# Sums of weight blocks made by accumulating DMAs on GpSimd's queue instead of by VectorE, in a transformer layer on Trainium2

## The chip, the cores and the metric

The kernel runs on one core of a Trainium2 chip, as one launch. The metric is device time in microseconds (us): the median of several executions. One further execution is recorded by the hardware profiler; its trace is what the prediction reads. The engines of the core each work through their own queue of instructions in a fixed order and wait on semaphores: TensorE (PE; its weight loads are listed as PEld), VectorE (DVE), ScalarE (ACT), GpSimd (POOL) and SyncE (SP). Before the change, SyncE issues every DMA of the kernel.

## The reference

One layer on a sequence of 1024 positions with 1024 channels, in float32:

```
h = rms_norm(x)
proj = h @ w_in                      # 1024 x 7168: q, k, v, gates, LRU branch, merge gates
A: rotary(q, k), chunkwise retention, group norm, swish gate, @ w_ret_o
B: causal conv (4), RG-LRU scan, times gelu(y), @ w_lru_o
x = x + (sigmoid(gate_A) * A + sigmoid(gate_B) * B) @ w_out
up = rms_norm(x) @ ffn_w_up          # 1024 x 6144
x = x + (gelu(conv3(gate)) * val) @ ffn_w_down
out = rms_norm(x)
```

## The kernel before, in words

**Tiles and units.** All large matrix products are cut into units (class `Job`). A unit computes a 256 x 1024 block of a product, as four quarters of 128 x 512, one per PSUM bank, from four weight blocks `A11`, `A12`, `A21`, `A22` of 128 x 512 values (256 KB each) and eight pairs of operand tiles. Float32 accuracy is kept with three passes: `split` (lines 617 to 621 of the kernel before) makes of a tile a rounded high half `hi` (a cast on ScalarE, L619) and a low half `lo = src - hi` (a subtraction on VectorE, L620), and TensorE multiplies hi by hi, hi by lo and lo by hi (L704 in seven-product units, L684 in plain ones).

**Seven-product units.** Most units use a scheme with seven block products instead of eight (`mm_fast`, Winograd's form of Strassen's). Each product is 12 matmuls of 128 x 512, so a unit is 84. The weight side needs `A11`, `A12`, `A22` and four sums: `S1 = A21 + A22`, `S2 = S1 - A11`, `S3 = A11 - A21`, `S4 = A12 - S2`. `blocks` (from L623) makes them on demand: SyncE loads a block (tile `wr`, L629), VectorE adds (S1 into a tile `ws` at L640, S2 in place at L643, S3 in place over `A11` at L646, S4 in place at L649), then `split` makes the halves. The order of the products in a unit is A11, S1, S2, A12, S3, S4, A22. Three banks X, Y, Z collect them: `keep` (L712, ScalarE) copies a bank to SBUF after the A11, S1 and S2 products, TensorE goes on accumulating on X after its copies, and `total` (L722, VectorE) adds a bank to a kept copy. The A22 product ends the unit and goes from the bank straight to `emit`. The activation side needs four sums T1 to T4, made once per operand by `tsets` or, through DRAM, by `sums_of` (lines 778 to 787).

**Stages.** Input projection: four plain units, then 24 seven-product units from about 103 us on; beside them run rotary embedding, retention heads and LRU blocks, as generators that are advanced after each product. Then the projections of both branches, `w_out` with plain units, FFN up (two plain units, 22 seven-product units from 971 us on) with convolution and gelu (tiles `gc`, stored to `ff_d`), and FFN down (12 seven-product units).

**What sets the order.** `record` writes down all operations; `Prog` then orders each engine's instructions with a list scheduler: each operation has a cost (`cost`), a latest start found backwards from TensorE's order (`plan`), and `forward` walks through time, giving every engine the ready operation with the earliest latest start, as long as one of 100 tile buffers of 128 x 512 is free. TensorE's main order is that of the recording. The instructions are then written in that order, and at run time an engine never passes over a waiting instruction.

Of the kernel before, what the change touches and what calls it, by code (L numbers as in the profile page):

```python
# [205 lines left out]
class Prog:  # L206
# [54 lines left out]
    def cost(self, o, how, n, outs, ins, args, kw):  # L261
# [25 lines left out]
        elif o.eng == "ACT":  # L287
            c = n / 1.2
            func = args[2] if how == "activation" else None
            o.tab = TABLES.get(func)  # L290
            extra = (60 if scal else 0) + (20 if func is not None else 0)
            o.occ, o.lat = c + (52 if ps else 95) + extra, c + (195 if ps else 230) + extra
            if "accum_out" in kw:
                o.occ += 150
                o.lat += 200
            o.occ += 20
        elif how == "dma_start":
            size = math.prod(args[0].shape) * 4
            o.dma = size
            o.occ = 420 if o.eng == "SP" else 800  # L300
            o.lat = 2700
        else:
            o.occ, o.lat = n * 2.0 + 100, n * 2.0 + 200
# [71 lines left out]
    def forward(self, caps):  # L375
# [37 lines left out]
        dma_free = 0.0  # L413
        tab = None
# [27 lines left out]
        def start(o, t):  # L442
            nonlocal dma_free, tab, slip, n
# [6 lines left out]
            if o.dma:  # L450
                arrive = max(t + 700, dma_free)
                dma_free = arrive + o.dma / 262144 * self.TILE
                lat = max(dma_free + 900 - t, 2300.0)
# [120 lines left out]
RATE = 2.5  # L574
SLACK = 45000.0
# [3 lines left out]
class Job:  # L579

    def __init__(self, src, op, emit, post=None, fast=True, pre=None, fetch=None, js=(0, 1, 2, 3)):
        self.src, self.op, self.emit, self.post = src, op, emit, post
        self.fast, self.pre, self.fetch = fast, pre, fetch
        self.js = js


def record(prog, fx):
# [35 lines left out]
    def blocks(jb):  # L623
        raw, blk = {}, {}

        def load(nm):
            if nm not in raw:
                t = get("wr")
                SY.dma_start(t, jb.src(int(nm[1]) - 1, int(nm[2]) - 1))  # L629
                raw[nm] = t  # L630
            return raw[nm]

        def block(nm):
            if nm in blk:
                return blk[nm]
            if not jb.fast or nm in ("A11", "A12", "A22"):
                s = load(nm)
            elif nm == "S1":
                s = raw["s"] = get("ws")
                V.tensor_add(s, load("A21"), load("A22"))  # L640
            elif nm == "S2":
                s = raw["s"]
                V.tensor_sub(s, s, raw["A11"])  # L643
            elif nm == "S3":
                s = raw["A11"]
                V.tensor_sub(s, s, raw["A21"])  # L646
            else:
                s = raw["s"]
                V.tensor_sub(s, raw["A12"], s)  # L649
            blk[nm] = split(s, "w")  # L650
            return blk[nm]

        return block
# [39 lines left out]
    def mm_fast(jb, op):  # L693
# [15 lines left out]
        def keep(ps):  # L709
            u = get("pk")  # L710
            with within(1200.0):
                S.copy(u, ps)  # L712
            return u

        def more(u, m, c):
            if jb.pre is not None and (m, c) in jb.pre:
                with within(3000.0):
                    V.tensor_add(u, u, jb.fetch(m, c))

        def total(u, ps, m, c):  # L720
            with within(1200.0):
                V.tensor_add(u, ps, u)  # L722
# [7 lines left out]
        z = keep(Z)  # L730
# [11 lines left out]
        with within(1500.0):  # L742
            jb.emit(1, 0, X, None)
# [30 lines left out]
    def sums_of(fetch, dst, j):  # L774
# [3 lines left out]
        V.tensor_sub(t, b[0, 1], b[0, 0])  # L778
# [5 lines left out]
        V.tensor_sub(b[1, 1], b[1, 1], t)  # L784
        SY.dma_start(dst[1, j], b[1, 1])
        yield 1.0
        V.tensor_sub(b[1, 0], b[1, 0], b[1, 1])
# [10 lines left out]
    def tsets(op, fetch):  # L798
        for j in range(4):
            b11, b12, b21, b22 = (fetch(n, j) for n in ("B11", "B12", "B21", "B22"))  # L800
            t1, t2 = get("ts"), get("ts")
            V.tensor_sub(t1, b12, b11)
            op["T1", j] = split(t1, "b")
            V.tensor_sub(t2, b22, t1)
# [3 lines left out]
            V.tensor_sub(t2, b21, t2)  # L808
# [141 lines left out]
    def emit_to(d, name, func=None):  # L950
        def emit(m, h, src, unit):
            t = get(name) if unit is None else unit
            if func is not None:
                S.activation(t, src, func)
            elif unit is None:
                S.copy(t, src)
# [3 lines left out]
    def emit_y(n):  # L960
        def emit(m, h, src, unit):
            t = get("y") if unit is None else unit
            S.activation(t, src, AF.Gelu_apprx_tanh)
# [169 lines left out]
    def emit_gate(which, n, scaled):  # L1133
        def emit(m, h, src, unit):
# [5 lines left out]
            S.activation(t, src, AF.Sigmoid, bias=pc("merge_gate_b", 8 * which + 2 * n + m))  # L1140
# [32 lines left out]

    def emit_ret_o(n):
        def emit(m, h, ps, unit):
            t = ojobs[n].fetch(m, h)
            V.tensor_mul(t, ps, t)
# [3 lines left out]
    def emit_lru_o(n):  # L1181
        def emit(m, h, ps, unit):
            g, t = ojobs[4 + n].fetch(m, h)
            V.tensor_mul(g, ps, g)
# [6 lines left out]
    def add(i, emit, post=None):  # L1191
        fast = len(jobs) >= STD_L
        jobs.append(Job(pair_src(w_in, i), h1 if fast else h1u, emit, post, fast=fast))
# [27 lines left out]
    ojobs = [Job(pair_src(w_ro, n), og, emit_ret_o(n), fast=n >= STD_RO, fetch=from_sg(0, n)) for n in range(4)]  # L1221
    ojobs += [Job(pair_src(w_lo, n), u, emit_lru_o(n), fast=n >= STD_LO, fetch=from_sg_t1(n))
# [19 lines left out]
    def emit_out(n):  # L1242
        def emit(m, h, ps, unit):
# [3 lines left out]
            V.tensor_add(t, ps, t)  # L1247
# [26 lines left out]
    def channel_major():  # L1274
# [9 lines left out]
        run([Job(pair_src(w_out, n), mop, emit_out(n), out_post(n), fast=n >= STD_W, js=(0, 1, 3, 2))  # L1284
# [63 lines left out]
    run([Job(pair_src(w_up, i), h2, emit_to(gvs[i], "gv"), up_post(i), fast=i >= STD_U) for i in range(NF)])  # L1348
# [15 lines left out]
    def emit_down(g, t):  # L1364
        def emit(m, c, src, unit):
            if unit is not None:
                acc = unit
            else:
                acc = djobs[4 * g + t].fetch(m, c)
                V.tensor_add(acc, src, acc)  # L1370
# [14 lines left out]
    def final(t, m):  # L1385
# [5 lines left out]
        for c in range(2):  # L1391
# [3 lines left out]
            else:  # L1395
# [4 lines left out]
                 emit_down(g, t), pre=((0, 0), (0, 1), (1, 1)), fetch=from_x1(t))  # L1400
# [98 lines left out]
```

## Time and profile before

| | |
|---|---|
| median of 3 runs | 1625.58 us (1625.5 to 1626.76) |
| profiled execution, its own time | 1628.01 us |
| its span in the trace | 1626.2 us |
| granted TensorE clock, mean | 0.999 |
| DMAs issued by SyncE | 1,054, 268.68 MB |
| VectorE instructions | 2,360 |

A line of the trace's groups reads: source line, engine, operation, output tile <- input tiles by their names in the program, shapes, xcount, then busy us in total, mean ns of one, and the engine's idle time just ahead of these instructions with what ended it. Line numbers are those of the kernel before, unless said otherwise; after the change `split` is L630 and L631, `keep` L735, `total` L749, the accumulating DMA L648.

### The profile page before, as it was taken

How to read it: one execution, taken by the hardware profiler on the slowest of the kernel's cores; microseconds unless marked ns; L12 is line 12 of the kernel's file. 1: busy time of each engine (PE TensorE's matmuls, PEld its weight loads, DVE VectorE, ACT ScalarE, POOL GpSimd, SP SyncE). 2: the span in 40 equal slices, each digit the busy share in tenths (PEclk: the TensorE clock that was granted, in tenths of full speed). 3: DMA queues.
4: the chain of work that ended last, by engine and by line, in shares of the span. 5: the costliest groups of instructions: out<-in, count | busy, mean ns of one | idle time of the engine just before them, and what ended most of it. 6: DMA issues, size and time to landing. Idle time of an engine off the chain costs nothing.

```text
span 1626.2 us, 21515 instructions
## 1 busy us (share of the span) xinstructions
PE 1603.8 (99%) x7204; PEld 1325.8 (82%) x7204; DVE 1294.9 (80%) x2360; ACT 925.9 (57%) x1592; POOL 0.2 (0%) x4
## 2 busy tenths in 40 slices
PE   7999999999999999999999999999999999999998
PEld 6888888888888888788888888888888888888886
DVE  4999668878779898989961599777777787989795
ACT  7764448749755866945430765444444455555564
POOL 0000000000000000000000000000000000000000
PEclk9999999999999999999999999999999999999999
DMA  9223304314225446999450514444444456987762
GB/s 334 85 98 107 88 27 137 106 38 159 76 90 182 150 154 209 320 370 345 136 206 0 174 54 141 151 142 144 148 130 138 146 163 196 335 287 273 271 237 97
DMA packets 167631, 270.04 MB, mean 166 GB/s; under 512 B 16864, under 2 KB 43616, under 8 KB 167520
## 3 DMA queue, kind: packets, MB, share of 16 engines
q1 hardware_dynamic: 167520, 268.68, 49.1%
q8 instruction: 56, 0.92, 0.2%
q14 instruction: 55, 0.45, 0.1%
HBM read 187.87 MB, written 75.50 MB: 162 GB/s over the span
## 4 chain that ended last, share of the span: by engine, by line
PE 91%; ACT 3%; DMA 3%; DVE 2%; issue 1%; SPq 0%; ACTq 0%; DVEq 0%
PE g L704 71%; PE g L684 14%; PE a L1001 2%; PE a L1094 1%; PE a L1093 1%; PE a L1101 1%; DMA bf<-u_d 1%; DMA wr<-w_lo 1%; DMA sg_d<-pk 0%; ACT L1004 0%; PE a L1124 0%; PE a L1087 0%; ACT L1014 0%; ACT lg L1004 0%; PE a L1254 0%
## 5 line engine op out<-in xcount | busy, mean ns | idle before, releaser
L704 PE MATMUL g<-bh,wl 128*128 128x512 f32 x1556 | 612.9, 394 | 0.4 <-DVE wl L620 0.4
L704 PE MATMUL g<-bh,wh 128*128 128x512 f32 x1556 | 612.2, 393 | 0.9 <-ACT pk L712 0.9
L704 PE MATMUL g<-bl,wh 128*128 128x512 f32 x1556 | 612.0, 393 | 0.0
L704 PEld LDWEIGHTS g<-bh,wh 128*128 128x128 f32 x1556 | 292.5, 188 | 60.4 <-ACT pk L712 1.5
L704 PEld LDWEIGHTS g<-bh,wl 128*128 128x128 f32 x1556 | 292.4, 188 | 60.5 <-DVE wl L620 1.2
L704 PEld LDWEIGHTS g<-bl,wh 128*128 128x128 f32 x1556 | 292.5, 188 | 59.5
L620 DVE TENSOR_TENSOR wl<-wr,wh 128x512 fp32r<-128x512 f32 x304 | 205.6, 684 | 19.5 <-ACT wh L619 18.9
L619 ACT CAST wh<-wr 128x512 fp32r<-128x512 f32 x304 | 180.6, 619 | 44.5 <-DVE wr L646 10.6
L722 DVE TENSOR_TENSOR pk<-g,pk 128x512 f32<-128x512 f32 x195 | 133.8, 686 | 81.5 <-PE g L704 80.9
L712 ACT COPY pk<-g 128x512 f32<-128x512 f32 x195 | 114.2, 586 | 139.5 <-PE g L704 136.5
L619 ACT CAST wh<-ws 128x512 fp32r<-128x512 f32 x195 | 120.8, 621 | 127.5 <-DVE ws L643 51.4
L620 DVE TENSOR_TENSOR wl<-ws,wh 128x512 fp32r<-128x512 f32 x195 | 133.2, 685 | 21.5 <-ACT wh L619 20.7
L704 PE MATMUL g<-hh,wl 128*128 128x512 f32 x264 | 102.8, 389 | 0.0
L704 PE MATMUL g<-hl,wh 128*128 128x512 f32 x264 | 102.8, 389 | 0.0
L704 PE MATMUL g<-hh,wh 128*128 128x512 f32 x264 | 102.8, 389 | 0.0
L684 PE MATMUL g<-hh,wh 128*128 128x512 f32 x192 | 76.7, 399 | 9.6 <-ACT wh L619 9.6
L1320 DVE SCALAR_TENSOR_TENSOR gc<-pk,par,gc 128x511 f32<-128x511 f32 x88 | 65.6, 746 | 23.0 <-ACT gc L1317 22.6
L1317 ACT ACTIVATE gc<-pk,par 128x512 f32<-128x512 f32 x44 | 35.9, 815 | 76.0 <-DVE pk L722 75.9
L684 PE MATMUL g<-hl,wh 128*128 128x512 f32 x192 | 76.4, 398 | 0.0
L684 PE MATMUL g<-hh,wl 128*128 128x512 f32 x192 | 76.3, 397 | 0.0
L684 PE MATMUL g<-bl,wh 128*128 128x512 f32 x160 | 63.2, 395 | 0.0
L684 PE MATMUL g<-bh,wl 128*128 128x512 f32 x160 | 63.1, 394 | 0.0
(236 smaller groups left out, 2134.7 us busy)
## 6 DMA issues: line engine op xcount, KB each, us to landing
wr<-w_in SPq DMA_DIRECT2D x112, 256.0 KB, 3.2
wr<-w_up SPq DMA_DIRECT2D x96, 256.0 KB, 3.5
dw<-w_dn SPq DMA_DIRECT2D x96, 256.0 KB, 5.0
ff_d<-gc SPq DMA_DIRECT2D x48, 256.0 KB, 2.5
wr<-ff_d SPq DMA_DIRECT2D x48, 256.0 KB, 5.1
td<-td_d SPq DMA_DIRECT2D x48, 256.0 KB, 5.3
x<-x_d SPq DMA_DIRECT2D x48, 256.0 KB, 5.2
td_d<-dw SPq DMA_DIRECT2D x36, 256.0 KB, 2.0
```

The source lines that it names most:

```text
L619: S.copy(hi, src)
L620: V.tensor_sub(lo, src, hi.bitcast(F32))
L684: PE.matmul(ps[m], w[a][:, c], o[b], start=k == 0 and i == 0, stop=k == 7 and i == 2)
L704: PE.matmul(ps, w[a][:, c], o[b], start=first and n == 0, stop=n == 11, skip_group_check=True)
L712: S.copy(u, ps)
L722: V.tensor_add(u, ps, u)
L1001: PE.matmul(ps, wg[g][a][:, cs], xs[k][b], start=q == 0, stop=q == 5)
L1093: PE.matmul(p2[:, 0:256], qk[0, h][:, bs], rst[cur], start=True, stop=False)
L1094: PE.matmul(p2[:, 0:256], s, v, start=first, stop=True)
L1101: PE.matmul(p3[:, 0:256], kd[h][:, bs], v, start=True, stop=True)
L1317: S.activation(c, src, AF.Identity, bias=pc("ffn_conv_b", i), scale=pc("ffn_conv_w", 48 + i))
L1320: V.scalar_tensor_tensor(c[:, s:], src[:, :TH - s], w, c[:, s:], ALU.mult, ALU.add)
```

## The change

In `blocks`, a unit can now ask for sums by DMA: an accumulating DMA issued from GpSimd adds a weight block from DRAM to a tile in SBUF. An addition is all that is used, so the sums change sign: `S2 = S1 + A11` and so on, with the signs turned on the activation side (`sums_of`, `tsets`), in `keep` (a copy with a scale of 1 or -1), in `total` and in the `emit` functions. The units of the input projection (`ACC_IN`) and of FFN up (`ACC_UP`) have all four sums made in this way; those of the other stages keep VectorE, with the new signs. S1 is made over the loaded `A21`, S2 and S4 on the same tile after it, S3 over `A11`. In each of these 46 units GpSimd issues four DMAs of 256 KB, 184 in all, and each of them waits until both halves of the block that stood in the tile have been made.

```
+ACC_IN = 2
+ACC_UP = 2
+ACC_DN = 0
+ACC_O = 0
...
+        def part(nm):
+            return jb.src(int(nm[1]) - 1, int(nm[2]) - 1)
+
+        def plus(t, nm):
+            G.dma_start(t, part(nm), accum_op=ALU.add)
+            return t
...
-            if not jb.fast or nm in ("A11", "A12", "A22"):
+            if nm[0] == "A":
                 s = load(nm)
-            elif nm == "S1":
-                s = raw["s"] = get("ws")
-                V.tensor_add(s, load("A21"), load("A22"))
-            elif nm == "S2":
-                s = raw["s"]
-                V.tensor_sub(s, s, raw["A11"])
-            elif nm == "S3":
-                s = raw["A11"]
-                V.tensor_sub(s, s, raw["A21"])
+            elif nm == "S3":
+                if jb.acc > 0:
+                    s = plus(raw["A11"], "A21")
+                else:
+                    s = raw["A11"]
+                    V.tensor_add(s, s, raw["A21"])
+            elif nm == "S1":
+                if jb.acc > 0:
+                    s = raw["s"] = plus(load("A21"), "A22")
+                else:
+                    s = raw["s"] = get("ws")
+                    V.tensor_add(s, load("A21"), load("A22"))
+            elif jb.acc > 1:
+                s = plus(raw["s"], {"S2": "A11", "S4": "A12"}[nm])
             else:
                 s = raw["s"]
-                V.tensor_sub(s, raw["A12"], s)
+                V.tensor_add(s, s, raw[{"S2": "A11", "S4": "A12"}[nm]])
...
-        def keep(ps):
+        def keep(ps, scale=1.0):
             u = get("pk")
             with within(1200.0):
-                S.copy(u, ps)
+                S.activation(u, ps, AF.Copy, scale=scale)
             return u
...
         def total(u, ps, m, c):
             with within(1200.0):
-                V.tensor_add(u, ps, u)
+                (V.tensor_sub if m else V.tensor_add)(u, u, ps)
...
-        V.tensor_sub(b[1, 1], b[1, 1], t)
+        V.scalar_tensor_tensor(b[1, 1], t, -1.0, b[1, 1], ALU.mult, ALU.subtract)
```

The scheduler's costs get a line for these DMAs (a higher latency, twice the bytes), so the order of all engines is made anew:

```
-            o.lat = 2700
+            o.lat = 2700 if "accum_op" not in kw else 4500
```

Three places of the new order, which the prediction uses. The names are tiles with a running number: `wr` a loaded weight block, `ws` a sum made by VectorE, `wh` and `wl` the halves of a block, `g` a PSUM bank, `pk` a kept copy, `gc` and `gv` gate and value tiles of FFN up, `lg`, `lth` and `ly` tiles of an LRU block.

**ScalarE, in the middle of FFN up.** Before the change, around the end of one unit and the start of the next (row 1110 takes the A22 product of one unit from its bank, row 1112 keeps the A11 product of the next):

```order
1108 L1317 ACTIVATE gc_10863<-pk_10803,par 128x512
1109 L619 CAST wh_10870<-wr_10850 128x512
1110 L956 COPY gv_10879<-g_10722 128x512
1111 L1323 ACTIVATE gc_10863<-gc_10863 128x512
1112 L712 COPY pk_10904<-g_10877 128x512
1113 L619 CAST wh_10909<-ws_10898 128x512
1114 L619 CAST wh_10927<-ws_10898 128x512
1115 L712 COPY pk_10934<-g_10902 128x512
```

After the change, at the like place (row 1110 takes the A22 product, rows 1106, 1112 and 1117 cast S1, S2 and S4 of one tile, row 1114 casts S3, row 1113 keeps the A11 product):

```order
1106 L630 CAST wh_10817<-wr_10775 128x512
1107 L630 CAST wh_10824<-wr_10801 128x512
1108 L1350 ACTIVATE gc_10830<-pk_10754,par 128x512
1109 L630 CAST wh_10845<-wr_10821 128x512
1110 L983 ACTIVATE gv_10850<-g_10686 128x512
1111 L1356 ACTIVATE gc_10830<-gc_10830 128x512
1112 L630 CAST wh_10867<-wr_10775 128x512
1113 L735 ACTIVATE pk_10873<-g_10842 128x512
1114 L630 CAST wh_10892<-wr_10821 128x512
1115 L735 ACTIVATE pk_10896<-g_10871 128x512
1116 L735 ACTIVATE pk_10918<-g_10842 128x512
1117 L630 CAST wh_10923<-wr_10775 128x512
```

The casts of the sums have moved among the copies out of PSUM, and one of them (row 1112) ahead of the copy that it used to follow. In every second unit the copy still comes first.

**VectorE, in an LRU block of the input projection.** Before the change, where the S4 block of one unit is summed (row 445) and its low half made (row 447); the addition that follows the A12 product of that unit, on bank `g_2873`, is row 467:

```order
443 L620 TENSOR_TENSOR wl_2729<-wr_2599,wh_2720 128x512
444 L722 TENSOR_TENSOR pk_2668<-g_2617,pk_2668 128x512
445 L649 TENSOR_TENSOR ws_2684<-wr_2735,ws_2684 128x512
446 L620 TENSOR_TENSOR wl_2757<-wr_2735,wh_2751 128x512
447 L620 TENSOR_TENSOR wl_2767<-ws_2684,wh_2759 128x512
448 L620 TENSOR_TENSOR wl_2781<-wr_2645,wh_2775 128x512
449 L1052 TENSOR_TENSOR pk_2405<-pk_2405,cos_1545 128x512
```

After the change, from the addition that follows the A12 product (row 418, on bank `g_2857`) to the low half of that unit's S4 block (row 427):

```order
418 L749 TENSOR_TENSOR pk_2773<-pk_2773,g_2857 128x512
419 L1053 TENSOR_TENSOR lg_2802<-lg_2802,lth_2784 128x512
420 L1081 TENSOR_TENSOR qk_2577<-qk_2577,qs_2822 128x512
421 L1055 SCALAR_TENSOR_TENSOR lg_2802<-lg_2758,lg_2802 128x512
422 L1081 TENSOR_TENSOR pk_2404<-pk_2404,qs_2837 128x512
423 L1043 SCALAR_TENSOR_TENSOR lg_2816<-lg_2816,lth_2846 128x512
424 L1057 SCALAR_TENSOR_TENSOR lth_2784<-lg_2758,st,lg_2802 128x512
425 L1044 TENSOR_SCALAR lg_2816<-lg_2816 128x512
426 L1062 TENSOR_TENSOR ly_2723<-ly_2723,lth_2784 128x512
427 L631 TENSOR_TENSOR wl_2920<-wr_2569,wh_2904 128x512
```

The low half has moved from 20 rows ahead of that addition to 9 rows behind it, after a scan (row 424) and other LRU and rotary operations. On TensorE, 8 transposes and 14 matmuls stand between the end of the product on `g_2857` and the first matmul that reads `wl_2920`.

**GpSimd, in FFN up.** Before the change GpSimd has no DMA. After it, its queue holds these and nothing else after the start; each unit is S1 and S2 on one tile (x2), S3 on another, S4 on the first:

```order
119 L648 DMA wr_10775<-w_up 128x512 x2
120 L648 DMA wr_10821<-w_up 128x512
121 L648 DMA wr_10775<-w_up 128x512
122 L648 DMA wr_10938<-w_up 128x512 x2
123 L648 DMA wr_10990<-w_up 128x512
124 L648 DMA wr_10938<-w_up 128x512
```

The sums of the next unit follow the S4 of this one directly, in the one queue.

More of the change, by code (lines that the diff above doesn't have):

```diff
@@ L716, in more @@
             if jb.pre is not None and (m, c) in jb.pre:
+                if jb.where is not None:
+                    with within(3000.0):
+                        G.dma_start(u, jb.where(m, c), accum_op=ALU.add)
+                    return
                 with within(3000.0):
```

89 lines of the change are left out of this document (51 added, 38 removed).

## The prediction, before the result was known

> **What bounds the kernel now.** I read the page's busy times first, then a table of stretches, then the waits of the engine that is busiest.
>
> ```profile
> span 1626.2 us, 21515 instructions
> PE 1603.8 (99%) x7204; PEld 1325.8 (82%) x7204; DVE 1294.9 (80%) x2360; ACT 925.9 (57%) x1592; POOL 0.2 (0%) x4
> 970.81 647.37 PE g L704 x2856
> ```
>
> The first two lines are from the page, the third from the chain of waits in order of time. TensorE is busy for all but 22.4 us, and the last 647 us before the tail are one unbroken piece of 2,856 matmuls: 647.37 / 2856 = 0.2267 us each. One product of a unit is 12 matmuls, 2.72 us; one seven-product unit is 84, 19.04 us. This pace does not depend on VectorE, so a lighter VectorE can only win back TensorE's gaps. Where those lie is in the stretches (length, busy time of PE, PEld, DVE, ACT, POOL, granted clock, DMA share, GB/s):
>
> ```profile
> 0.00:103.00 103.00, 93.39 (x402) 76.11 (x403) 76.71 (x143) 72.55 (x138) 0.20 (x4) 1.00 0.52 183
> 103.00:196.00 93.00, 93.00 (x414) 77.03 (x414) 75.13 (x149) 39.94 (x66) 0.00 (x0) 1.00 0.34 99
> 196.00:330.00 134.00, 132.85 (x618) 109.64 (x617) 103.92 (x201) 90.86 (x138) 0.00 (x0) 1.00 0.28 89
> 330.00:490.00 160.00, 160.00 (x747) 132.84 (x746) 122.16 (x249) 103.06 (x158) 0.00 (x0) 1.00 0.28 91
> 490.00:664.00 174.00, 171.38 (x792) 141.45 (x791) 154.40 (x308) 121.48 (x185) 0.00 (x0) 1.00 0.55 187
> 971.00:1390.00 419.00, 419.00 (x1851) 347.21 (x1850) 336.44 (x561) 211.88 (x357) 0.00 (x0) 1.00 0.47 153
> 1618.00:1627.00 9.00, 0.17 (x1) 0.00 (x0) 3.31 (x15) 3.07 (x7) 0.00 (x0) 0.71 0.31 117
> ```
>
> The change acts in the seven-product units of the input projection (103 to 664 us) and of FFN up (971 to 1390). In these TensorE's gaps are 1.15 + 2.62 = 3.77 us, all in the projection; in FFN up there is none. The other gaps (start, middle, tail) are in work that keeps its operations. So nothing that the change frees can be worth more than 3.77 us, 0.23% of the profiled execution's 1628.0 us. Who causes these gaps, from TensorE's waits in 103 to 664 us:
>
> ```profile
> PE a L1001 <- ACT lg L1004: 1.1, 1, 1.1
> PE a L1101 <- DVE state L1103: 0.9, 1, 0.9
> PE g L704 <- ACT pk L712: 0.9, 1, 0.9
> PE a L1001 <- DVE xsl L620: 0.6, 1, 0.6
> ```
>
> None names a weight-block sum (`ws` or `wr` on VectorE): they are hidden today.
>
> **The change part by part.** *Removed:* four VectorE sums in each of 46 units (24 in the projection, 22 in FFN up).
>
> ```profile
> L646 DVE TENSOR_TENSOR wr<-wr,wr 128x512 f32<-128x512 f32 x65 | 44.6, 686 | 0.9
> L643 DVE TENSOR_TENSOR ws<-ws,wr 128x512 f32<-128x512 f32 x65 | 44.6, 686 | 1.5 <-DMA wr<-ff_d 0.6
> L640 DVE TENSOR_TENSOR ws<-wr,wr 128x512 f32<-128x512 f32 x65 | 44.3, 682 | 10.7 <-DMA wr<-w_in 7.8 <-issue 1.7 <-DMA wr<-w_up 1.2
> L1016 DVE SCALAR_TENSOR_TENSOR lg<-lg,lth 128x512 f32<-128x512 f32 x16 | 10.9, 684 | 11.4 <-ACT lg L1014 11.4
> ```
>
> 184 x 0.685 = 126 us of VectorE time goes, all beside TensorE's matmuls: 0 taken, -3.77 us at best.
>
> *Signs:* a subtraction that becomes a `scalar_tensor_tensor` costs the same (684 against 682 to 686 above): 0. `keep`, the copy of a PSUM bank, becomes an ACTIVATE with a scale. Its old row, the nearest row of the new form, the cast and the gelu on the same engine:
>
> ```profile
> L712 ACT COPY pk<-g 128x512 f32<-128x512 f32 x195 | 114.2, 586 | 139.5 <-PE g L704 136.5
> L1062 ACT ACTIVATE kd<-a,cst 128x512 f32<-128x512 f32 x8 | 5.5, 683 | 0.0
> L619 ACT CAST wh<-ws 128x512 fp32r<-128x512 f32 x195 | 120.8, 621 | 127.5 <-DVE ws L643 51.4 <-DVE ws L640 42.9 <-DVE ws L649 25.3
> L1323 ACT ACTIVATE gc<-gc 128x512 f32<-128x512 f32 x48 | 30.3, 632 | 45.8 <-DVE gc L1320 39.4 <-DVE gc L1322 5.7
> ```
>
> At most 0.10 us per copy, 195 x 0.10 = 19 us of an engine that is 57% busy; one product of 2.72 us covers a copy. 0 taken; without cover it would be those 19 us.
>
> *The new order on VectorE* (second place shown in the section on the change). In the LRU stretch row 427 makes `wl_2920`, the low half of the block that TensorE needs two matmuls into its next product but one. Ahead of it stand rows 418 to 426: seven plain operations, a scan and a `tensor_scalar`; row 418 itself waits for the end of the product on `g_2857`.
>
> ```profile
> L1030 DVE TENSOR_TENSOR_SCAN lth<-lg,st,lg 128x512 f32<-128x512 f32 x8 | 10.2, 1277 | 0.0
> L1017 DVE TENSOR_SCALAR lg<-lg 128x512 f32<-128x512 f32 x16 | 6.7, 420 | 0.1
> 766.27 0.68 DVE L1185 TENSOR_TENSOR t1l<-t1l,sgl 128x512 f32<-128x512 f32 x1
> 766.87 0.68 DVE L722 TENSOR_TENSOR pk<-g,pk 128x512 f32<-128x512 f32 x1
> 908.36 0.87 PE a L1254 x8
> ```
>
> Two neighbours in the timeline start 0.60 us apart, 0.08 less than one lasts. So row 427 is done after 7 x 0.60 + (1.28 - 0.08) + (0.42 - 0.08) + 0.68 = 6.4 us. TensorE has until then eight 128x128 transposes (0.87 us for eight in the chain) and 14 matmuls (3.17): 4.0 us. It stands for 2.4 us. A second run of this kind, rows 767 to 778 ahead of `wl_5319` with two scans, takes 8 x 0.60 + 2 x 1.20 + 0.34 + 0.68 = 8.2 us against 12 matmuls and 16 transposes, 4.5: between 0 and 3.7 us, by how far TensorE has run ahead when it begins; I take 2.0. Together **+4.4 us**. In the order before, the block for the first place is made 20 rows ahead of the row that stands where row 418 now does.
>
> *The accumulating DMAs.* 184 of them, 256 KB each, go through GpSimd's queue, which issues none today. No row of the trace is one, so their time from issue to landing, L, has to be bounded. Loads of the same blocks by SyncE (median us to landing is last), and the DMA engines when nearly full:
>
> ```profile
> wr<-w_in SPq DMA_DIRECT2D x112, 256.0 KB, 3.2
> wr<-w_up SPq DMA_DIRECT2D x96, 256.0 KB, 3.5
> dw<-w_dn SPq DMA_DIRECT2D x96, 256.0 KB, 5.0
> 0.00:40.00 40.00, 30.39 (x121) 23.88 (x122) 16.72 (x37) 28.11 (x63) 0.20 (x4) 1.00 0.97 339
> ```
>
> From below: no dearer than a load, 3.5 us. From above: two loads one after another, 7.0. An accumulate also reads its destination out of SBUF and sends the sum back: two passes of 0.262 MB at 339 GB/s, 0.77 us each. I take L = 3.5 + 1.54 = 5.0, near the 5.0 of loads that wait among others.
>
> What hides L? S1, S2 and S4 are made on one tile, one on top of the other: each must land, be cast by ScalarE (0.62) and subtracted by VectorE (0.68) before the next may be issued, 1.30 us per step beside L. If nothing of a unit overlapped the next, a unit's chain would be a load and three steps, 3.5 + 3 (L + 1.30) = 19.04, full at L = 3.9. If S4's landing and the load lie wholly beside the next unit, it is 2 (L + 1.30) = 19.04, full at L = 8.2. GpSimd's rows put S1 of the next unit straight behind S4, and the loads stand in SyncE's queue behind `ff_d` stores that themselves wait for a gelu behind a cast, so part overlaps: with half of the third step counted, 3.5 + 2.5 (L + 1.30) = 19.04 gives L = 4.9. This half is my choice, an estimate.
>
> Who passes the lateness on is ScalarE (first place in the section on the change): the cast of `wh_10867`, which now waits for a landing, stands in front of the copy `pk_10873`, and TensorE reuses that bank one product later. Of those 2.72 us the cast and the copy take 0.62 + 0.59, so a cast that waits over 1.5 us longer than the product holds TensorE up. Before, no cast of a sum stood there. At L = 5.0 the chain is over its unit by 2.5 x (5.04 - 4.91) = 0.33 us, 46 x 0.33 = **+15 us**; at L = 3.5 it is 0, at 7.0 it is 46 x 2.5 x 2.1 = 241.
>
> *Traffic:* 184 x 0.262 = 48 MB more reads. In FFN up 88 x 0.262 MB over 419 us is 55 GB/s; at today's 0.47 of the engines for 153 GB/s that is 0.17 more, 0.34 if it counts double: 0.81 at most, so it makes landings later (it is in L) but is no bound by itself. SyncE keeps the number of its DMAs.
>
> **Sum.** 1628.0 (the profiled execution; its span 1626.2 and 1.8 around it) + 4.4 + 15 = 1647.4. The median of the runs, 1625.58, lies 2.4 below the profiled execution, so the forecast is **1645 us**. A measurement of this kernel tells about 0.2% (3.3 us) from no change.
>
> **The rivals.**
>
> *Landings are quick.* If an accumulate costs hardly more than a load (L of 3.5 to 4.9), the chain is covered and only VectorE's two crowded places are left: 1625.6 + 4.4 = 1630, slower by 0.27%. For it: loads of `w_in` land in 3.2 us while the DMA engines are 0.28 to 0.55 busy. Against it: GpSimd's path and the adding are both without a row. The Trainium skill's page "DMA: Bandwidth & Descriptors", section "Anatomy of one DMA — SWDGE (gpsimd) path", fits a plain DMA from GpSimd as about 2.0 us plus its bytes at 436 GB/s, an estimate of 2.6 us here, under the 3.5 of the row; by it L would be 4.1 and the time this rival's. No run yet shows such a DMA.
>
> *The order's stalls only replace old ones.* The 3.77 us of gaps in these stretches come from the same LRU and retention work; if they go and 4.4 come, +0.6: 1626, no change. It needs quick landings as well.
>
> *Faster.* VectorE, freed of 126 us in stretches where it is 76 to 89% busy (122.16 of 160, 154.40 of 174), reaches the LRU work sooner; all 3.77 us go and nothing comes in: 1621.8. It decides only if L stays under 4.9 and the crowded places are met with TensorE's weights two products ahead. Against it: rows 418 to 427 are in the order whatever L is.
>
> *The chain becomes the bound.* L over 5.5, because accumulates share the engines with bursts of loads: 46 x 2.5 x (5.5 - 4.91) = 68 us, so 1625.6 + 4.4 + 68 = 1698 and more. For it: the 5.0 us of `dw` loads shows what bursts do to landings. The Trainium skill's page "SBUF — State Buffer", section "SBUF: two separate sides", speaks against the change too: it warns that GpSimd cannot write descriptors while VectorE runs an operation in a mode that takes both ports. In these stages such an operation would be a `tensor_scalar` of 0.42 us (row above), which only the LRU stretch has; no run shows it, and nothing is added for it.
>
> **How the numbers follow.** Forecast (L of 4.9 to 5.5: 1630 to 1698) 0.45; quick landings (1629 to 1631) 0.25; replaced stalls (1626) 0.10; faster (1622) 0.04; chain over 1698 0.16. Slower by over 0.2% is the first, second and last, 0.86; within 0.2% 0.10; faster 0.04. The range leaves out the fastest and the slowest case, 0.20: 1625 to 1700.
>
> **What would show it.** Right: in the profile after, `wh<-wr` casts on ScalarE wait for `wr` DMAs in place of `ws` sums, TensorE waits for ScalarE's copies (now L735) in FFN up, where it had no wait at all; VectorE loses 126 us; accumulates land after about 5 us. Two waits of about 2 us for a `wl` in the LRU stretch would show the order's part. Wrong: TensorE without gaps in 971 to 1390 us, or landings below 4.5 us with gaps all the same, which would put the cause elsewhere; or gaps of over 1.5 us per unit, which would make L or the number of serial steps larger than taken.

## The result, and the profile after

The changed kernel takes 1684.68 us (median of 4 runs, 1682.26 to 1692.77) against 1625.85 us before on the same chip: the ratio is 1.037, 95% interval 1.0352 to 1.0389. The forecast was 1645. The direction was right; the loss, 58.8 us, is three times the forecast one, and the question is which term of the sum was too small.

The page's first lines, after (own time of the profiled execution 1685.55 us):

```profile
span 1683.8 us, 21875 instructions
PE 1625.0 (97%) x7204; PEld 1330.3 (79%) x7204; DVE 1181.8 (70%) x2176; ACT 919.2 (55%) x1591; POOL 160.7 (10%) x188
```

VectorE lost 184 instructions and 113 us, and nothing came of it. TensorE is idle for 58.8 us (by chance the same number as the loss) where it was for 22.4 (36.4 more), and *busy* for 21.2 us longer with the same 7,204 matmuls, which needs an explanation of its own (below).

The stretches, with the columns of the table in the prediction:

```profile
103.00:196.00 93.00, 90.40 (x396) 73.84 (x396) 60.53 (x125) 36.98 (x62) 14.71 (x16) 1.00 0.64 149
196.00:330.00 134.00, 131.13 (x603) 107.67 (x602) 87.86 (x175) 83.06 (x129) 17.70 (x21) 0.99 0.52 120
330.00:490.00 160.00, 155.44 (x701) 126.70 (x699) 96.71 (x189) 98.67 (x150) 23.14 (x27) 0.99 0.58 132
490.00:690.00 200.00, 195.06 (x895) 160.01 (x895) 157.71 (x324) 133.51 (x205) 22.57 (x26) 0.99 0.79 218
1010.00:1200.00 190.00, 177.14 (x756) 143.11 (x755) 108.49 (x185) 80.98 (x138) 32.05 (x37) 0.98 0.71 176
1200.00:1440.00 240.00, 226.86 (x974) 183.67 (x973) 144.71 (x246) 110.71 (x189) 36.33 (x42) 0.99 0.76 197
```

The gaps are in every stretch with accumulating DMAs, most of all in FFN up, which had none before: 12.86 us of 190 and 13.14 of 240. The DMA engines are busy for at most 0.79 of a stretch: they are not full. Of the lines of TensorE's waits these are the four longest, and below them the two longest of ScalarE's on DMAs (us in total, times, longest):

```profile
PE g L727 <- DVE pk L749: 24.7, 17, 3.2
PE g L707 <- ACT wh L630: 8.8, 2, 7.0
PE g L727 <- ACT pk L735: 8.2, 8, 2.2
PE g L727 <- DVE wl L631: 5.4, 4, 2.5
```

```profile
ACT wh L630 <- DMA wr<-w_up: 120.4, 62, 7.3
ACT wh L630 <- DMA wr<-w_in: 111.1, 55, 6.7
```

The 8.8 us are the start of the kernel, as before (9.6 there). No line of TensorE's waits names a DMA: ScalarE's casts wait for landings, 231.5 us in all (loads and accumulates), and TensorE waits for what stands behind them, the totals of VectorE (`pk`, L749) and the copies of ScalarE (`pk`, L735). What a landing takes, from the page's DMA issues (the last number is the median from issue to landing) and, from the view of line 648, who waited for the accumulates and their minimum, median and maximum to landing:

```profile
wr<-w_in SPq DMA_DIRECT2D x112, 256.0 KB, 4.3
wr<-w_in POOLq DMA_DIRECT2D x96, 256.0 KB, 5.0
wr<-w_up SPq DMA_DIRECT2D x96, 256.0 KB, 4.6
wr<-w_up POOLq DMA_DIRECT2D x88, 256.0 KB, 5.2
```

```profile
who waited for it (us, times):
  ACT wh L630: 208.7, 97
...
DMA to landing us min/median/max: 3.8/5.1/9.5
```

Of ScalarE's waiting 208.7 us are for accumulates, 97 waits in 46 units. L was taken rightly: 5.0 predicted, 5.1 measured. The loads beside the accumulates land 1.1 us later than before.

One pause of FFN up, in the chain that ended last (start us, length us, what; "issue" as in the page's legend):

```profile
1272.52 5.03 DMA wr<-w_up
...
1277.59 5.70 issue
1283.30 4.14 DMA wr<-w_up
1287.46 0.63 ACT wh L630
1288.12 0.70 DVE wl L631
...
1289.10 7.23 DMA wr<-w_up
1296.35 0.63 ACT wh L630
...
1298.22 0.69 DVE ds L805
1298.90 0.60 DVE pk L749
...
1301.49 0.61 DVE pk L749
...
1302.14 7.38 PE g L727 x24
```

S1 lands at 1277.55, but S2 may be issued on the tile only at 1283.30, 5.70 us later (1.30 had been taken), because S1's halves are made when the queues of ScalarE and VectorE come to them. From S2's landing to the issue of S4 it is 1.64 us. S4 lands after 7.23 us; its cast and its `wl` stand ahead of the totals, and TensorE, which needs a bank back, starts again at 1302.14.

What follows that pause is in TensorE's timeline (start, length, in brackets the wait ahead):

```profile
1302.14 0.50 PE L727 MATMUL g<-bh,wh 128*128 128x512 f32 x1 [2.33 <-DVE pk L749]
...
1302.71 0.42 PE L727 MATMUL g<-bh,wl 128*128 128x512 f32 x1
1302.94 0.62 PE L727 MATMUL g<-bh,wh 128*128 128x512 f32 x1
1303.35 0.63 PE L727 MATMUL g<-bl,wh 128*128 128x512 f32 x1
1303.78 0.63 PE L727 MATMUL g<-bh,wl 128*128 128x512 f32 x1
```

The starts were 0.227 us apart and are 0.43 from 1302.94 on, for eight matmuls: by the trace's record of the clock the granted clock is at half for 3.41 us. This happens 7 times between the start and the tail, 7 x 3.41 / 2 = 12 us, and makes most of the 21.2 us by which TensorE is longer busy; the other 9 are not resolved (ends of matmuls are modelled).

### The profile page after: what moved, and what is told of

It is laid out like the page before. It is cut to its first block, busy times and chain, and to the rows that moved or that the text cites. A ratio compares the mean times of both kernels' runs of the same rounds, so it can differ in the third digit from the quotient of the medians.

```text
span 1683.8 us, 21875 instructions
## 1 busy us (share of the span) xinstructions
PE 1625.0 (97%) x7204; PEld 1330.3 (79%) x7204; DVE 1181.8 (70%) x2176; ACT 919.2 (55%) x1591; POOL 160.7 (10%) x188
## 5 line engine op out<-in xcount | busy, mean ns | idle before, releaser
L727 PE MATMUL g<-bh,wh 128*128 128x512 f32 x1556 | 620.2, 399 | 33.3 <-DVE pk L749 24.7
L631 DVE TENSOR_TENSOR wl<-wr,wh 128x512 fp32r<-128x512 f32 x442 | 298.3, 686 | 260.5 <-ACT wh L630 250.8
L630 ACT CAST wh<-wr 128x512 fp32r<-128x512 f32 x442 | 264.2, 616 | 268.4 <-DMA wr<-w_up 120.4
L735 ACT ACTIVATE pk<-g 128x512 f32<-128x512 f32 x195 | 115.0, 595 | 114.3 <-PE g L727 112.2
L749 DVE TENSOR_TENSOR pk<-pk,g 128x512 f32<-128x512 f32 x195 | 132.9, 682 | 47.5 <-PE g L727 46.6
L648 POOL DMA_DIRECT2D wr<-w_up x88 | 76.2, 881 | 672.2 <-DMA wr<-w_up 386.1
L648 POOL DMA_DIRECT2D wr<-w_in x96 | 84.3, 921 | 576.4 <-DVE wl L631 295.4
L1353 DVE SCALAR_TENSOR_TENSOR gc<-pk,par,gc 128x511 f32<-128x511 f32 x88 | 65.7, 746 | 16.6 <-ACT gc L1350 16.5
L707 PE MATMUL g<-bh,wh 128*128 128x512 f32 x160 | 62.7, 392 | 0.0
```

The source lines that it names most:

```text
L630: S.copy(hi, src)
L631: V.tensor_sub(lo, src, hi.bitcast(F32))
L648: G.dma_start(t, part(nm), accum_op=ALU.add)
L707: PE.matmul(ps[m], w[a][:, c], o[b], start=k == 0 and i == 0, stop=k == 7 and i == 2)
L727: PE.matmul(ps, w[a][:, c], o[b], start=first and n == 0, stop=n == 11, skip_group_check=True)
L735: S.activation(u, ps, AF.Copy, scale=scale)
```

## The experiments

Two theories stand at the start. **Chain**: three landings of 5 us, one after another on one tile, do not fit into a unit of 19.04 us; fewer serial steps or fewer DMAs help. **Traffic**: 48 MB more make all landings later, whatever waits for them. A third was put on record beside them, before any of these runs. **Order**: the list scheduler takes a time of its own for such a DMA, 4.5 us in its due times and 3.5 or more in its walk through time (below); it puts the casts where these landings would be, and every landing that comes later stops engines that work in order.

All medians, and where the time goes. The last five columns are the start of one matmul, counted from the first one, less that of the same matmul before (us, one trace of each kernel; matmul 1200 starts at 277 us before the change, 1600 at 365, 3200 at 717, behind the projection; 4400 at 982 and 6000 at 1345, at the two ends of FFN up's seven-product units).

| kernel | us | ratio to before (95%) | 1200 | 1600 | 3200 | 4400 | 6000 |
|---|---|---|---|---|---|---|---|
| changed | 1684.68 | 1.037 (1.0352 to 1.0389) | 3.4 | 8.4 | 20.0 | 19.6 | 57.9 |
| signs only | 1628.65 | 1.0019 (1.001 to 1.0029) | -1.0 | -0.9 | -2.4 | -1.2 | -1.2 |
| S1 and S3 only by DMA | 1694.9 | 1.0434 (1.041 to 1.0458) | 5.5 | 8.7 | 16.6 | 17.1 | 74.8 |
| idle accumulates | 1642.24 | 1.0098 (1.0081 to 1.0115) | 1.0 | 2.3 | 6.9 | 13.3 | 15.2 |
| idle copies | 1632.0 | 1.004 (1.0025 to 1.0055) | 0.0 | 0.8 | 4.9 | 3.5 | 5.2 |
| order for 2 us | 1721.45 | 1.0602 (1.0579 to 1.0625) | 13.8 | 17.9 | 32.5 | 32.7 | 101.9 |
| order for 6 us | 1641.24 | 1.0098 (1.0083 to 1.0113) | 0.4 | 5.3 | 8.0 | 6.4 | 11.3 |
| order for 10 us | 1635.66 | 1.0062 (1.0046 to 1.0079) | -0.6 | 6.1 | 4.1 | 7.7 | 9.1 |
| S1 and S3, order for 6 us | 1632.11 | 1.0044 (1.0029 to 1.0059) | -0.1 | 3.5 | 1.3 | 5.1 | 5.1 |
| FFN up only, 6 us | 1633.77 | 1.0051 (1.0036 to 1.0066) | 0.6 | 0.6 | -0.1 | 0.2 | 8.0 |
| projection only, 6 us | 1636.6 | 1.0073 (1.0056 to 1.009) | -0.8 | 5.3 | 9.7 | 8.6 | 8.7 |
| a quarter of the bytes | 1630.63 | 1.0035 (1.0021 to 1.0049) | -0.7 | 0.5 | 1.9 | 1.6 | 3.1 |
| a quarter of the bytes, 6 us | 1633.05 | 1.005 (1.0035 to 1.0065) | 0.0 | 5.0 | 6.5 | 4.9 | 4.9 |

The kernel before, run beside each of them, had medians of 1624.73 to 1625.85 us.

**Signs only.** No accumulating DMA, the signs, the `keep` with a scale and the new order as they are:

```
-ACC_IN = 2
-ACC_UP = 2
+ACC_IN = 0
+ACC_UP = 0
```

> All sums stay on VectorE (no accumulating DMA); only the turned signs and the scaled copies are left, and the order is made anew. Chain theory (the loss comes from landings that later steps wait for): no change, 1624 to 1629 us. Traffic theory (the loss comes from 48 MB more on the DMA engines): the same, 1624 to 1629. If the turned signs or the scaled copies cost anything, this run shows it: 195 copies x up to 0.1 us would be up to 19 us.

Measured 1628.65 us, 3.4 above before. The interval of the ratio does not hold 1, but the executions lie between 1625.9 and 1629.64, and the traced one, the fastest, shows no place for the loss. The DMAs, with the order made for them, are the loss.

**One serial step less.** S1 and S3 by DMA, S2 and S4 on VectorE: 92 DMAs, and no accumulate waits for another on the same tile.

```
-ACC_IN = 2
-ACC_UP = 2
+ACC_IN = 1
+ACC_UP = 1
```

> S1 and S3 by accumulating DMA, S2 and S4 by VectorE on top of S1: half of the DMAs (92), and one landing in a unit's chain in place of three. Chain theory: a chain of one load, one landing and two additions is 3.5 + 6.4 + 2 x 2 = 14 us, under the unit's 19, so most of the loss goes: 1628 to 1640 us. Traffic theory: half of the loss stays, 1650 to 1660 us.

Measured 1694.9 us, 10 *more* than with all four. This is a miss for both theories: the chain has one landing instead of three, and half the bytes are added. The longest of TensorE's waits, and the landings, of this kernel:

```profile
PE g L727 <- ACT pk L735: 39.4, 18, 4.5
```

```profile
DMA to landing us min/median/max: 3.8/4.6/8.2
```

Landings are earlier than in the changed kernel, and TensorE waits more for the copies out of the banks. What is late is late against the place that the order gives it (the table below has the times), not against the length of a chain.

**Traffic alone.** All sums on VectorE; the 184 DMAs run beside them onto tiles that are no longer needed, once as accumulates and once as plain copies from GpSimd's queue. The lines of the accumulates (for the copies, each `plus(t, nm)` is `G.dma_start(t, part(nm))`; in both, `ACC_IN` and `ACC_UP` are 1 and only mark the units):

```
+            if jb.idle and nm == "S3":
+                plus(raw["A21"], "A22")
+                plus(raw["A11"], "A21")
+            if jb.idle and nm == "S4":
+                plus(raw["A12"], "A12")
+                plus(raw["s"], "A11")
```

> All sums on VectorE, but GpSimd issues the same number of accumulating DMAs (184, same size, same kind) onto tiles whose contents are dead, so that nothing reads what they add (their values do not enter the output). Chain theory: nobody waits for a landing, so 1626 to 1636 us, with loads landing about 1 us later as in the changed kernel. Traffic theory: most of the 58 us is back, 1665 to 1685 us.

> All sums on VectorE, and 184 plain copies of 256 KB from GpSimd's queue onto dead tiles that nothing reads (they do not enter the output), in place of 184 accumulating DMAs (1642 us). If the 16 us of that run come from bytes on the DMA engines whatever their kind: 1636 to 1644 us. If they come from the second pass of an accumulate: 1627 to 1635 us, and landings of loads nearer to 3.2 us.

Measured 1642.24 us, between the two expected ranges, and 1632.0. The DMA rows of the accumulates, then those of the copies (the tiles named `ws` have rows of their own):

```profile
wr<-w_in POOLq DMA_DIRECT2D x72, 256.0 KB, 4.7
wr<-w_up POOLq DMA_DIRECT2D x66, 256.0 KB, 5.2
```

```profile
wr<-w_in POOLq DMA_DIRECT2D x72, 256.0 KB, 3.3
wr<-w_up POOLq DMA_DIRECT2D x66, 256.0 KB, 3.7
```

With the full traffic and landings as late as in the changed kernel, but nobody waiting for them, TensorE loses 1.9 us in FFN up (13.3 to 15.2 in the table), where the changed kernel loses 38.3. Traffic by itself is not the loss there. Some 13 us are lost ahead of FFN up, in single places (between matmuls 2400 and 2800, and 3200 and 3600). Since the scheduler counts an accumulate's bytes twice, the two kernels' orders differ too. In the walk of the accumulates' kernel TensorE waits 5.3 us at 756 us, where the trace has two pauses (3.5 us to 769.8, 2.8 to 772.6); in the copies' walk it does not. So part of the 10 us between the two is order; how much is bytes stays open. The copies give the price of the adding: about 1.5 us more to landing.

**The order, and nothing else.** The same DMAs and the same arithmetic; only the times (in ns) that the scheduler takes for an accumulate are altered, here to 6 us and more; two more kernels have 12000, 2500 and 10000 in the same places ("10 us") and 2700, 0 and 2300 ("2 us"):

```
-            o.lat = 2700 if "accum_op" not in kw else 4500
+            o.lat = 2700 if "accum_op" not in kw else 7000
...
-                    lat = max(acc_free + 900 - t, 3000.0)
+                    lat = max(acc_free + 2500.0 - t, 6000.0)
```

> The changed kernel with one thing altered: the scheduler is told that an accumulate lands after at least 6 us (before: 3.0) and 2.5 us after its bytes (before: 0.9), so it issues them earlier and places the casts later. Same DMAs, same three steps in a unit's chain. If the loss comes from an order that has the casts waiting ahead of copies (order theory): most of it goes, 1628 to 1645 us. If three landings of 5 us in a row are too long for a unit of 19 us whatever the order, or if traffic is the cause: 1670 to 1690 us.

> All four sums by DMA, ordered for landings after at least 10 us instead of 6. Order theory: landings take 3.8 to 9.5 us, median 5; the few above 6 are covered now, so a few us less than at 6: 1632 to 1642 us. If what is left at 6 us (16 us over the kernel before) is traffic, it does not move: 1638 to 1644 us.

> All four sums by DMA, ordered for landings after at least 2.3 us (the changed kernel: 3.0, with a later end of its bytes added). Order theory: every cast is placed still earlier and waits longer: 1700 to 1780 us. If the order's expectation does not matter, and the order for 6 us helped by chance: 1640 to 1690 us.

These numbers are least values, and in the early orders they are never reached. In the walk an accumulate counts for twice its bytes, 1600 ns, behind a start of 1000 and, in the changed kernel, with 900 behind it: 3500 at the least, not 3000. Where another DMA is still under way the 1600 count twice, 5100 in all, and accumulates close behind one another take up to 9500. The table sets the walk's times for the accumulates, as the scheduler of each kernel works them out, against the landings in its trace, each DMA against its own time in the walk (us):

| kernel | walk: least, median, mean | landing: median, mean | later than in the walk | us over before |
|---|---|---|---|---|
| order for 2 us | 2.6, 4.2, 3.9 | 5.0, 5.3 | 160 of 184 | 96 |
| changed | 3.5, 5.1, 4.8 | 5.1, 5.4 | 133 of 184 | 59 |
| order for 6 us | 6.0, 6.7, 6.8 | 5.0, 5.3 | 35 of 184 | 16 |
| order for 10 us | 10.0, 10.0, 10.0 | 4.9, 5.2 | 0 of 184 | 11 |
| S1 and S3 only by DMA | 3.5, 3.5, 4.0 | 4.6, 5.0 | 73 of 92 | 70 |
| S1 and S3, order for 6 us | 6.0, 6.0, 6.3 | 4.4, 4.9 | 11 of 92 | 7 |
| a quarter of the bytes | 3.5, 5.1, 4.8 | 3.0, 3.5 | 27 of 184 | 6 |
| a quarter of the bytes, 6 us | 6.0, 6.7, 6.8 | 3.0, 3.4 | 2 of 184 | 8 |

So the walk's typical time was right for the changed kernel, 5.1 against 5.1. What it had wrong is which DMA takes how long, and it left no margin: 80 of the 184 were taken at 3.5 us and landed after 4.3 as a median, 101 at 5.1 or more and landed after 5.9. An order with a margin of some 1.5 us on the mean loses far less. Due times and walk were always altered together; which of the two does it is not shown.

The orders for 2, 3 (the changed kernel), 6 and 10 us take 1721, 1685, 1641 and 1636 us. FFN up's stretch, the landings, and ScalarE's and TensorE's waits in the order for 6 us:

```profile
960.00:1440.00 480.00, 477.12 (x2096) 392.44 (x2095) 332.22 (x564) 243.27 (x411) 74.62 (x86) 1.00 0.79 211
```

```profile
DMA to landing us min/median/max: 3.8/5.0/9.4
```

```profile
ACT wh L630 <- DMA wr<-w_up: 59.0, 45, 3.9
ACT wh L630 <- DMA wr<-w_in: 46.4, 30, 4.0
...
PE g L727 <- DVE wl L631: 5.0, 2, 2.7
PE g L727 <- ACT wh L630: 2.6, 1, 2.6
PE g L727 <- DVE pk L749: 2.4, 4, 1.0
```

The landings are the same (3.8/5.0/9.4 against 3.8/5.1/9.5), three of them still follow one another in a unit, and the chain fits: 477.12 us of 480 are busy. ScalarE waits 105.4 us for landings instead of 231.5, TensorE 2.4 us for the totals instead of 24.7. That is 43 us of the 58.8, from two lines that do not change a single DMA.

**One step, in the order for 6 us.** Both edits together (`ACC_IN` and `ACC_UP` 1, and the two lines above).

> S1 and S3 by accumulating DMA, S2 and S4 by VectorE, as in the run that came out at 1694.9 us, but ordered for landings after at least 6 us. Order theory: the loss of that run came from casts placed right behind an expected landing, so it goes here as it did with three steps: 1628 to 1642 us. If instead VectorE's additions on top of a DMA's sum are the trouble: 1670 us or more.

Measured 1632.11 us. With the early order it took 10 us more than four DMAs per unit, with the late order it takes 9 less (1641.24 less 1632.11). The number of DMAs and of serial steps counts only once the order is right.

**The same order, earlier landings.** The counterpart: the order of the changed kernel, the same rows on TensorE, ScalarE, VectorE and SyncE, and shorter DMAs, in it and in the order for 6 us: each adds 32 of the 128 partitions, so that three quarters of every sum are left out.

```
-            args = [a.ap() if isinstance(a, Ref) else a for a in o.args]
+            args = [(a.ap()[0:32, :] if "accum_op" in o.kw else a.ap()) if isinstance(a, Ref) else a for a in o.args]
```

> The changed kernel's order, row for row on every engine; each accumulating DMA adds only 32 of the 128 partitions (64 KB of 256), so three quarters of each of these sums are missing. Theory (the order puts casts where a landing after some 3 us would be, and landings come after 5): if the landings fall to 3 or 3.5 us, the same order costs little, 1630 to 1640 us; at 4 us about 1650; if they stay at 5, nothing is learned. Rival (the new order is bad whatever the landings are): 1670 to 1685 us with landings of 3.5 us or less.

> The same quarter of the bytes in the order made for 6 us, whose full run took 1641.24. If what is left there above before comes from bytes and late landings, it goes to near the run with signs alone: 1629 to 1632 us. If it comes from the crowded places of that order in the projection, where VectorE makes the low half late whenever the DMA lands: 1634 to 1640 us, with the pauses near 323, 326 and 593 us again.

In the changed kernel's order it is 1630.63 us. Its landings, FFN up and TensorE's longest wait after the start:

```profile
DMA to landing us min/median/max: 2.4/3.0/7.2
```

```profile
960.00:1440.00 480.00, 479.51 (x2113) 395.93 (x2112) 336.23 (x571) 243.79 (x416) 64.47 (x84) 1.00 0.60 178
```

```profile
PE g L727 <- DVE wl L631: 5.0, 4, 2.1
```

Most landings now come before the time that the walk has for them (27 of 184 are later, 133 in the changed kernel), and of the 58.8 us 5.9 are left. The order is not bad in itself and the landings of 5 us are not too late in themselves: the loss comes from landings behind their places in the order. That fewer bytes alone would have done it is excluded in FFN up: with all bytes, the idle accumulates lose 1.9 us there and the order for 6 us 4.9, against 38.3. In the order for 6 us the quarter takes 1633.05 us, between the two expectations: FFN up is free of gaps (4.9 and 4.9 in the table), and the 5.0 us at matmul 1600 stay, as they do with all bytes (5.3 less 0.4).

**One stage alone, in the order for 6 us.** `ACC_IN = 0`, then `ACC_UP = 0`.

> The order made for 6 us (as in the 6-us run, 1641.24), but accumulating DMAs only in FFN up (88 of the 184); the projection's sums stay on VectorE. If what is left of the 6-us run (some 16 us above before) sits in the projection's crowded places, where the trace of the 6-us run shows three pauses of over 2.6 us (323.0, 326.3, 593.5), nothing of them is left here: 1626 to 1632 us. If it is the traffic, spread over all units alike, about half of it is left: 1633 to 1636 us.

> The other half: the order made for 6 us, accumulating DMAs only in the projection (96 of the 184), FFN up's sums on VectorE. If the rest sits in the projection's crowded places: 1636 to 1642 us, with the pauses near 323, 326 and 593 us again. If it is traffic, spread evenly over the units: 1633 to 1636 us.

Measured 8.6 and 11.5 us above before; less 3.4 for the signs it is 5.2 and 8.1, and with the 3.4 they add up to 16.7, as the kernel with both stages shows (16.0). Neither theory has it alone. Where each loses shows in these rows: with DMAs only in the projection, its LRU stretch and the last unbroken piece, which began at 970.81 before; with DMAs only in FFN up, that stage:

```profile
196.00:330.00 134.00, 129.16 (x590) 106.29 (x590) 86.90 (x174) 83.09 (x128) 16.65 (x20) 0.97 0.51 125
...
978.84 647.42 PE g L727 x2856
```

```profile
960.00:1440.00 480.00, 474.96 (x2083) 389.73 (x2082) 329.85 (x561) 240.26 (x408) 71.74 (x83) 1.00 0.79 211
```

In the first all is lost ahead of FFN up, most of it in single places near 314, 317 and 587 us of the span (the expectations' 323, 326 and 593 are 316, 318 and 586 in the span of the order for 6 us); in the second there is no pause of over 1.5 us in the stage, and 5.04 us of short waits, which go with a quarter of the bytes and shrink with a later order (1.4 us between matmuls 4400 and 6000 in the order for 10).

## Why the prediction was right or wrong

**Nothing to gain: right.** No kernel here is below before. VectorE's busy time fell by 113 us, not by 126: the prediction counted each sum at its full 0.685 us, but an operation starts before the one ahead of it has ended (0.60 us apart, as the prediction's own rows show), so each takes only 0.61 us of busy time with it.

**L = 5.0 us, worked out between 3.5 and 7.0: right,** 5.1 as a median (mean 5.4). The price of the adding, 1.54 us by the prediction's two passes, was about 1.5. The Trainium skill's page "DMA: Bandwidth & Descriptors", section "Anatomy of one DMA — SWDGE (gpsimd) path", has a fit that gives an estimate of 2.6 us for a plain DMA of this size from GpSimd. The copies landed after 3.3 and 3.7 us in a loaded kernel and the accumulates after 5.0 and 5.2, so the measurement decides against the rival built on it.

**VectorE's crowded places, 4.4 us (2.4 and 2.0): right.** In the changed kernel TensorE waits for a `wl` for 2.05 us until 322.2 and for 2.49 us until 596.4; from the start of row 418 to the end of row 427 it is 6.41 us, and 6.4 were worked out. With landings of 3.0 us in this very order the two waits are 2.06 and 2.05 us, and TensorE's lateness grows by 1.2 and 3.4 us in the stretches that hold them (from matmul 1200 to 1600, and from 2400 to 2800).

**ScalarE passes lateness on: right in kind, and only half of it.** The casts wait for landings, and copies behind them are late (8.2 us of TensorE's waits). VectorE passes on three times as much: the `wl` of a late cast stands in front of the totals (24.7 us). The prediction had looked at the row of ScalarE alone.

**GpSimd held up by VectorE: nothing of weight seen.** The prediction gives operations of the kind of `tensor_scalar` to the LRU stretch alone; the projection has them in rotary and the group norm too. In the changed kernel 19 issues on GpSimd overlap one: 13 of these took 0.86 or 0.87 us, the median of all, and the longest 1.19. No issue took over 1.25 us, so a hold-up of issues is at most 0.4 us.

**The chain, "2.5 (L + 1.30) is over its unit by 0.33 us, 46 x 0.33 = +15 us": this is the step that failed.** It compared the length of a chain with the length of a unit, as if only a chain that is too long could cost time. With the measured L it would have given 24 x 2.5 x (5.0 - 4.91) + 22 x 2.5 x (5.2 - 4.91) = 21 us, 16 of them in FFN up, where 38.3 are lost. But it is not a small error of size. With the mean landing of 5.4 us in place of the medians the same formula gives 46 x 2.5 x (5.4 - 4.91) = 56 us, near the measured loss, and that would be luck: with the mean of 5.3 in the order for 6 us it gives 45, where 16 are lost. The order for 6 us keeps three landings of 5 us per unit and loses 4.9 us in FFN up; the kernel with one landing in the chain loses 57.7 there. The "half of the third step" that overlaps, marked as a choice, is no property of the unit: the order decides it, and it had been made for landings after 3.5 to 9.5 us, 4.8 on the mean, of which 133 of 184 came later, by 0.65 us over all on the mean. The prediction named L = 5.0 and never set it against the times that the scheduler took. The two typical values would have agreed; what shows the loss is that the order took 3.5 us for some DMAs and left no margin for any. ScalarE reaches a cast before its accumulate has landed 97 times in 46 units, 2.2 us early on average (208.7 / 97), and each time what stands behind it in two queues is held up; TensorE feels it where a copy or a total is among that.

**The step of 1.30 us** failed with it, in the one place looked at: cast and subtraction last that long, but between S1's landing and the issue of S2 lie 5.70 us in the chain shown above, because both wait for their turn.

**What was left out: the clock.** The sum priced a pause at its own length. Pauses of over 2.2 us mostly (47 of 63) also halve the granted clock for the next 3.41 us, 1.7 us more each, 12 us in the changed kernel.

**Signs, 0 us: 3.4 were measured,** 0.19% (interval 0.10 to 0.29), so they are small and not nothing; the copy with a scale takes 0.595 us against 0.586 (195 x 0.009 = 1.8 us of ScalarE). Whether these 3.4 us are the new form of the copies or the new order stays open. **Traffic, no bound by itself: right for FFN up** (1.9 us with idle accumulates), open for the 13 us ahead of it.

The measured time lies inside the stated range, in the band with the chance of 0.45, and L inside that band's condition. The mechanism named for the band does not carry it there, as said: that the number fits the band is luck.

Of the forecast's loss, then, 4.4 us were sized well and the 15 should have been some 50. The changed kernel's 58.8 us are about 43 that an order for 6 us takes away, 3.4 with the signs, and some 12 that are left: the crowded places that also the new orders have, and short waits in FFN up that go with the bytes. A part of this the scheduler knew: by its own walk the span is 6.1 us longer in the changed kernel's order than in the one before (1620.8 against 1614.7) and 7.7 and 10.0 longer in those for 6 and 10 us, none of it in FFN up. The walk's places and the trace's agree only in part, so it is not shown that these are the same microseconds.

## What to carry to other kernels

Where a scheduler has ordered the engines, a new asynchronous step costs time wherever it ends later than the scheduler took for it and an in-order engine meets it there. Before working out chains, compare the two times, and not only the typical ones, which agreed here: compare them one DMA at a time, and give the order a margin (here 6 us for landings of 5). A kernel that loses time in this way is told by long waits of an engine off the bound for landings, passed on by the instructions behind them, and is tested from both sides: the same DMAs in an order for a longer time, and the same order with shorter DMAs. Moving work off an engine that is 80% busy gains nothing when the engine that bounds the kernel hardly waits for it, and here no order made the move pay.

## What the runs showed of the hardware

**Pauses and the clock.** Over the 14 traces of these kernels, counted by the starts of neighbouring matmuls: no pause of 1.4 to 1.8 us was followed by matmuls at half the pace (0 of 23), nor of 1.8 to 2.2 by itself (1 of 9, and in that one a pause of 4.2 us came right behind), 14 of 24 of 2.2 to 2.6, 12 of 14 of 2.6 to 3.0, 4 of 8 of 3.0 to 3.4, and all 17 longer ones. What decides between pauses of one length is in the traces' record of the clock: its stretches at full and at half clock are whole multiples of 3.413 us long (to 0.01 us), so the clock is set on a fixed grid and not when a pause ends. Sorted by TensorE's idle time within one window of that grid at full clock (from 50 us to 12 us before the end), all 43 windows with 1.85 us or more were followed by one at half clock, and none of the 6,393 with 1.82 or less. A pause of 3.2 us that the grid cuts in two halves can cost nothing more, one of 2.3 us inside a window costs 1.7 more. The Trainium skill's page "TensorE: Matmul & The Clock Gate", section "What's actually happening", has the clock go to half after an idle window of about 3.4 us; the width of the grid agrees with such a window, but in these traces it need not be idle throughout.

**Accumulates and their neighbours.** An accumulating DMA of 256 KB from GpSimd landed after 3.8 us at least, 5.1 as a median and 9.5 at most; one of 64 KB over 32 partitions after 2.4, 3.0 and 7.2. Loads that SyncE issues beside them land later, `w_in` after 4.3 us instead of 3.2 and `w_up` after 4.6 instead of 3.5.
